# The relative-bias table of a streaming encoder step: written by one DRAM-to-DRAM broadcast, with the far bias put in by a predicated copy

## The chip, the cores and the metric

The kernel runs on one core of one Trainium2 chip. The metric is the device time of one execution in microseconds. The kernel before takes 1836.98 us (median of 3 runs, 1836.38 to 1841.36). In the profile the engines are PE (matmul) and PEld (its weight load), DVE, ACT, POOL and SP; SP and ACT also issue the transfers between DRAM and the on-chip memory, and an instruction that only issues one is marked SPq or ACTq.

## The reference, cut to what matters

One layer of an encoder runs over 512 prompt tokens and 8 x 16 sample tokens. Branch A of it is banded attention with 8 heads of 64; to each score a bias is added that depends on the head and on the clipped distance between query and key:

```python
A_MAX_REL = 128                      # 257 biases per head

def rel_bias_lookup(table, rel):
    idx = jnp.clip(rel, -A_MAX_REL, A_MAX_REL) + A_MAX_REL
    return jnp.transpose(table[idx], (2, 0, 1)).astype(jnp.float32)

# band_attn_prompt, per chunk of 64 queries and head
s = jnp.einsum('bqhd,bkhd->bhqk', qb, kb).astype(jnp.float32) * scale + bias
p = jax.nn.softmax(jnp.where(valid, s, neg), axis=-1)
```

So a key more than 128 positions back gets one constant per head, the far bias. Everything else (the projections of branches A, B and C, the gated delta rule, the state-space scan, the merge, cross attention and the feed-forward part) is the same before and after the change.

## The kernel before

The tokens lie in five tiles of 128 (four of the prompt, one of the sample). Dense products are made in three passes over a high and a low part of each operand: a weight tile of 512 KB is loaded from DRAM into a tile called `raw` (L273; two such buffers in turn), ACT makes its high part `wh` (L224, two instructions of 128x512 per tile), POOL makes its low part `wl` from both (L218, two of 128x512), and PE multiplies (L210). A `raw` buffer is free for the next load when its two `wl` are done. There are buffers for three such tiles' `wh` and for as many `wl`; a further one is free when PE has used the oldest.

The order of the program is written by generators that take turns: a list of dense units (`add`, `need`, `pump`), and beside them the steps of other work. A recording layer then puts the instructions of each engine in a row; each engine runs its row strictly in that order and waits at the head of it.

Around the change the units are: V (values of all heads, products `tm`), A0 (queries and keys of head pair 0, products `aps`, results in `aqk`), dec (a small product `dps` with 24 weight columns, loaded into a tile `rawd` that takes one of the two `raw` buffers), then A1, A2, A3 (the other head pairs; each first its queries, then its keys). The keys' result is copied from PE's memory to `aqk` by ACT and then transposed by PE (`t5a`, `t5b`). The result of `dps` goes through ACT to `dsb` and is transposed in the same way, after the first product of A1.

Between V and A0 `rel_table` (L422) makes a table in DRAM, `relt`: for each of 128 queries q and 8 heads a row of 384 numbers, 127 copies of the far bias and then the 257 biases by falling distance. The 257 columns are loaded for 8 partitions (one per head), DVE fills in the 127 copies, and one store issued from ACT writes all 128 copies of the 8 rows:

```python
self.store(self.relt.rearrange("q h c -> h q c"), t.unsqueeze(1).broadcast_to([8, P, 384]))
```

`rel_ap` (L431) reads it back with a step of one number less than a row from query to query, which yields the bias per query and key. `prompt_bias` (L1302) makes the bias tile of two heads so: a load of 128x256 from `relt`, a POOL copy that spreads column 256 (the far bias) over columns 0 to 255, and a DVE memset of the corner that is masked. It is called before the attention (for pair 0) and then once for each later pair. `attn_sample` (L1369) reads small pieces of `relt` for the sample's 16 queries and spreads the far bias in the same way (L1377).

Of the kernel before, what the change touches and what calls it, by code (L numbers as in the profile page):

```python
# [7 lines left out]
F32 = mybir.dt.float32  # L8
F32R = mybir.dt.float32r
I32 = mybir.dt.int32  # L10
# [9 lines left out]
NT = 5            # token tiles: 4 of the prompt, 1 with the 8 x 16 sample tokens  # L20
# [5 lines left out]
NEG = -3.0e38  # L26
FA, FS, FB, FC, FP, FX = 0.3, 0.85, 0.95, 1.8, 1.2, 0.5
NGA, NGB, NGC = 5, 3, 5    # gates of the branches done ahead
# [4 lines left out]
SEQ = (0, 1, 2, 4, 3)   # tiles of a group's scan  # L33
LQ = 1
SKA = 3           # softmax tiles ahead of their products
MAGIC = float(0x5F3759DF)

NU = 41           # working slots of 128 x 640
NQ = 16           # of 128 x 128
NW = 6            # half weight tiles, and as many for the low parts  # L40
NS = 17           # small slots


class Enc:
# [39 lines left out]
    # Dense products come as units (generators that yield the time their products hold the tensor  # L84
    # engine); the steps of other work yield how much dense work is to be put behind them.
# [3 lines left out]
    def tick(self):  # L89
        """Next step of the work behind every finished product."""  # L90
        self.posts = [p for p in self.posts if next(p[1], self) is not self]
        for name in [n for n in self.ended if all(p[0] != n for p in self.posts)]:
            self.ended.remove(name)
            self.done.add(name)

    def post(self, gen):
        """First step of the work behind a product; the others come with later products."""
        if gen is not None and next(gen, self) is not self:
            self.posts.append((self.units[0][0] if self.units else None, gen))
# [34 lines left out]
    def weave(self, *gens, lead=0):  # L134
        """Steps of the generators in turn, the first one lead steps ahead."""
# [14 lines left out]
    def fmj(self, wk, X, post, m=P, c=0, nm="fm", split=False):  # L150
        """A weight-stationary product and the steps behind it."""
# [16 lines left out]
    def tmj(self, wk, X, cb, tiles=range(NT), nm="tm", t0=0, late=False):  # L168
        """cb(pair, ps[128 tokens, j, 256]): X^T (weights), per pair of token tiles; X starts at tile t0.
        late: the last row block comes after the others of the first two pairs."""  # L170
# [33 lines left out]
    def load2(self, out, in_):  # L204
        """A load that does not queue behind those of the weights."""
        self.nc.sync.dma_start(out, in_)

# [24 lines left out]
    def split(self, h, l, x, eng=None):  # L232
        """x = h + l exactly, both with 12 significant bits."""
        self.act(h, x)
        self.tt(l, x, h.bitcast(F32), ALU.subtract, eng)

    def rsqrt(self, v_in, scale, eps, post=1.0):
        """post / sqrt(v_in * scale + eps), elementwise on a small tile."""
# [18 lines left out]
    def sumsq(self, x, acc):  # L257
        """acc[p] = sum over the free axis of x*x."""
# [5 lines left out]
    def weights(self, w, c0, width, k0, nk, engs=None, loose=False):  # L264
        """Columns c0..c0+width of row blocks k0..k0+nk as [(h, l)] per row block."""
# [46 lines left out]
    def masks(self):  # L312
        nc = self.nc
        self.one = self.ones("one")
        self.mi = self.ones("mi")                             # [k, i] = 1 for k <= i
        self.keep(self.mi, [[1, P]], 0, -1)
        self.ms, blk = self.ones("ms"), self.Q("blk")         # [k, j] = 1 for k > j, within blocks of 16
# [7 lines left out]
        self.blkc = self.C("blkc", [P, 8])                    # [token, b] = 1 in block b  # L325
# [4 lines left out]
    def levels(self):  # L330
        """[j, i] = 1 where i lies in the upper half and j in the lower half of one block of 2s."""
        nc = self.nc
        self.par = self.C("par", [P, 2])                      # parity of the block of 16
        nc.vector.tensor_reduce(self.par, self.blkc.rearrange("p (a c) -> p c a", c=2), axis=AX.X, op=ALU.add)
        # packed: the diagonal blocks of 32 side by side
# [22 lines left out]
    def loads(self):  # L358
        """Loads of the small parameters and the convolutions' states."""
        I = self.I  # L360
        # vectors over features
# [14 lines left out]
        # parameters per head, on all partitions  # L376
# [16 lines left out]
    def params(self):  # L393
        nc = self.nc
        # vectors transposed; conv taps and gate gains come halved
# [26 lines left out]
    def rel_table(self):  # L422
        """DRAM scratch [q, head, 384]: 127 times the far bias, then the biases by falling distance; read
        with a partition step one short of a row it yields the band's bias per (query, key)."""
        self.relt = self.dr.tile([P, 8, 384], F32, name="relt")
        t = self.U("rel", shape=(8, 384))
        self.load(t[:, 127:384], self.I["a_rel_rev"])
        self.nc.vector.tensor_copy(t[:, 0:127], t[:, 127:128].broadcast_to([8, 127]))
        self.store(self.relt.rearrange("q h c -> h q c"), t.unsqueeze(1).broadcast_to([8, P, 384]))

    def rel_ap(self, h, nq, c0, n):  # L431
        """[nq, n]: bias of query q and key column c0 + c, column 128 being the query tile's first key."""
        return bass.AP(tensor=self.relt.tensor, offset=self.relt.offset + h * 384 + 127 + c0,
                       ap=[[8 * 384 - 1, nq], [1, n]])

# [9 lines left out]
    def XT(self, nm):  # L445
        """Feature-major halves of all tokens: [(h, l)] per feature tile."""
# [3 lines left out]
    def token_norm(self, xs):  # L450
        """[128, n]: 1 / rms of the tokens of n tiles, each given as two halves."""
# [7 lines left out]
    def inv_rms(self, ss):  # L459
        """[128, n]: 1 / rms from the parts' sums of squares, [128, parts, n]."""  # L460
# [20 lines left out]
    def norm_tile(self, x, r, g):  # L481
        """Normalized halves of a token tile, transposed to psum: yields (j, psum [128, 4, 128])."""
# [8 lines left out]
    def norm_T(self, x, gain, to, groups=((0, 1), (2, 3), (4,))):  # L491
        """x[t]: two [128, 512] tiles; fills the feature-major halves of all tokens."""
# [25 lines left out]
    def conv(self, ps, key, f, hist, taps, bias, lt):  # L518
        """ps: [128, 2, 320] pre-conv; returns views (prompt, sample) of x/2 of the conv result.
        The streams' last tokens, their new state, go to column lt[1] of the batch lt[0] of lt[2]."""  # L520
# [35 lines left out]
    def store_conv(self, lt, cols, hist, op, os):  # L556
        """The batch's new states: row (f, token) of the prompt, then (f, stream, token)."""
# [12 lines left out]
    def decays(self, X):  # L570
# [4 lines left out]
        # 24 columns count, 8 more fill up a quarter of the array  # L575
        for c, c0, n in ((0, 3072, 8), (8, 6152, 16), (24, 3080, 8)):
            self.load(raw[:, :, c:c + n], wv[:, :, c0:c0 + n])
        # a quarter of the array for every two row blocks; their sums come with the transposes
# [15 lines left out]
    def decays_post(self, sb):  # L594
# [6 lines left out]
        # beta = sigmoid  # L601
# [3 lines left out]
        # softplus(x) = max(x, 0) + log1p(exp(-|x|)), log1p(e) = 2 atanh(e / (2 + e))  # L605
# [24 lines left out]
        # sums of the decays: up to a token, after a token, whole tile  # L630
# [27 lines left out]
        # the sums up to a token once more, a row per head, to be read by all partitions  # L658
# [6 lines left out]
    def decay(self, out, ts, hs, eng=None):  # L665
        """out[j, i], the sums of the decays up to token i for tiles ts or heads hs, become the decays from
        token j to i, where i >= j (and at most 1 elsewhere)."""
# [8 lines left out]
    def tr5(self, src, cols=None):  # L676
        """src(t) -> [128, 128]; returns two psum tiles, prompt [128, 512] and sample [128, 128]."""
# [7 lines left out]
    def gdn_dense(self, h, X):  # L685
# [7 lines left out]
        def post(kind):  # L693
            f = kind * 4 + h

            def run(ps):
                c = self.silu_conv(ps, "b", f, 3, [self.vc("bcw", i * 12 + f) for i in range(4)], None,
                                   (lt, kind, 3), "bc")
                if kind < 2:
                    # k and q stay as they are: what their l2 norms would scale goes by token  # L700
# [17 lines left out]
                if kind == 0:  # L718
# [3 lines left out]
                    self.stt(sc[:, 0, :], ss[:, NT:], EPS, rk, ALU.add, ALU.mult)       # 1 / rk  # L722
# [23 lines left out]
        for kind in (1, 0, 2):                                # k, q, v  # L746
# [4 lines left out]
    def gdn_solve(self, h):  # L751
        """Decays, both products with the keys, and the inverse of I + strictly upper part."""
# [11 lines left out]
        # decays between the tokens of a tile, [j, i]  # L764
# [28 lines left out]
        # E = (I + U)^-1 for U = strictly upper part, by doubling the block size; up to 32 on the diagonal  # L793
        # blocks alone, which lie packed side by side
# [24 lines left out]
        for i in range(1, 5):  # L819
            n = NT if i < 4 else 4                            # the sample's blocks are of 16 tokens  # L820
# [8 lines left out]
        # the blocks above the diagonal: -A^-1 B D^-1  # L829
# [34 lines left out]
    def gdn_run(self, h):  # L864
        """Per tile: w = E^T z, outputs and state; then norm over the head and gate."""
# [11 lines left out]
        # z = v - e^gc (k s0), w = E^T z, o = e^gc (q s0) + M^T w, state  # L877
# [60 lines left out]
        # norm over the head, gate, to feature-major halves  # L938
# [997 lines left out]
```

## Time and profile before

| | us |
|---|---|
| median of 3 runs | 1836.98 |
| range of the runs | 1836.38 to 1841.36 |
| span of the profiled execution, first to last instruction | 1828.0 |
| PE busy in it | 1727.6 (95%) |
| DVE, ACT, POOL busy | 866.0, 652.7, 612.5 |

For the profiled execution the profile gives the span alone; the runs' median lies 9.0 us above it, which is what stands around the first and the last instruction. A row of a timeline begins with its start and its duration in us; a bracket at its end gives how long the engine sat idle before it and who ended that. The chain of waits is followed back from the last instruction: each piece is the work, or the transfer, that held the end at that moment. [...] A DMA share is the mean busy share of 16 DMA engines.

### The profile page before, as it was taken

To read this page: it belongs to the slowest core of one execution; us is meant where nothing else is said; L and a number is where in the kernel's file an instruction comes from. 1 tells how busy PE (TensorE), PEld (TensorE's weight loads), DVE (VectorE), ACT (ScalarE), POOL (GpSimd) and SP (SyncE) were. 2 spreads that over 40 slices of the span, in tenths; PEclk is the share of its full clock that TensorE was granted. 3 is DMA by queue.
4 is the path that set the end of the run, shared out by engine and by line. 5 is a ranking of instruction groups with operands and counts; after the bars stand their busy time and mean duration, and the time that the engine had idled before them with its cause. 6 is when DMAs were issued, how large, how long until landed. Compare 5 with 4: busy or idle time off the path is not lost.

```text
span 1828.0 us, 34046 instructions
## 1 busy us (share of the span) xinstructions
PE 1727.6 (95%) x13705; PEld 1593.3 (87%) x13705; DVE 866.0 (47%) x1778; ACT 652.7 (36%) x1611; POOL 612.5 (34%) x644
## 2 busy tenths in 40 slices
PE   6589999999999999999999899999989999999997
PEld 6587777889888887988989899987689999999997
DVE  5034655255777674665544463342474413431433
ACT  4034444432533442343342255332433312321333
POOL 4151222212332353453333236211144433433433
PEclk9889999999999999999999999999989999999999
DMA  5341127522221343234223435146332222222322
GB/s 156 64 113 54 49 70 243 184 67 61 78 76 52 98 121 115 72 110 133 78 68 92 138 126 164 58 162 230 105 93 82 70 71 81 75 66 70 93 77 76
DMA packets 239308, 182.41 MB, mean 100 GB/s; under 512 B 13313, under 2 KB 211982, under 8 KB 239150
## 3 DMA queue, kind: packets, MB, share of 16 engines
q1 hardware_dynamic: 216192, 164.69, 29.2%
q10 hardware_dynamic: 22958, 15.54, 3.3%
q8 instruction: 108, 1.77, 0.4%
q14 instruction: 50, 0.41, 0.1%
HBM read 162.04 MB, written 16.58 MB: 98 GB/s over the span
## 4 chain that ended last, share of the span: by engine, by line
PE 78%; DVE 10%; DMA 5%; ACT 3%; issue 2%; POOL 1%; ACTq 0%; SPq 0%; POOLq 0%; DVEq 0%
PE ups L210 8%; PE fps L210 8%; PE gps L210 8%; PE dn L210 8%; PE pps L210 6%; PE ap L210 6%; PE tm L210 4%; PE bps L210 4%; PE qps L210 3%; DMA raw<-in_w_in_dram 3%; PE cps L210 2%; PE aps L210 2%; DVE xc L221 2%; DVE t L218 1%; PE asp L210 1%
## 5 line engine op out<-in xcount | busy, mean ns | idle before, releaser
L218 POOL TENSOR_TENSOR wl<-raw,wh 128x512 fp32r<-128x512 f32 x376 | 494.5, 1323 | 1029.1 <-ACT wh L224 761.3
L224 ACT ACTIVATE wh<-raw 128x512 fp32r<-128x512 f32 x400 | 248.3, 629 | 606.2 <-PE dn L210 94.3
L210 PE MATMUL dn<-wh,hh 128*128 128x256 f32 x440 | 125.1, 284 | 0.4
L210 PE MATMUL dn<-wl,hh 128*128 128x256 f32 x440 | 124.7, 283 | 0.5 <-POOL wl L218 0.5
L210 PE MATMUL dn<-wh,hl 128*128 128x256 f32 x440 | 124.5, 283 | 0.0
L210 PE MATMUL gps<-xTh,wh 128*128 128x320 f32 x448 | 114.7, 333 | 1.8 <-DVE tg L221 1.8
L221 DVE SCALAR_TENSOR_TENSOR xc<-xp,vec,xc 128x664 f32<-128x664 f32 (+1 forms) x116 | 113.9, 982 | 3.1
L210 PE MATMUL gps<-xTl,wh 128*128 128x320 f32 x448 | 106.0, 314 | 0.0
L210 PE MATMUL gps<-xTh,wl 128*128 128x320 f32 x448 | 105.9, 314 | 0.0
L541 DVE TENSOR_SCALAR xc<-xp,vec 128x656 f32<-128x656 f32 (+1 forms) x34 | 32.2, 946 | 133.3 <-ACT xp L224 133.3
L210 PEld LDWEIGHTS dn<-wh,hh 128*128 128x128 f32 x440 | 84.4, 192 | 1.2 <-DVE x L218 1.0
L210 PEld LDWEIGHTS dn<-wl,hh 128*128 128x128 f32 x440 | 84.4, 192 | 0.9 <-POOL wl L218 0.9
L210 PEld LDWEIGHTS dn<-wh,hl 128*128 128x128 f32 x440 | 84.4, 192 | 0.0
L210 PEld LDWEIGHTS gps<-xTh,wh 128*128 128x128 f32 x448 | 72.9, 189 | 12.3 <-issue 9.1
L210 PE MATMUL fps<-fTh,wh 128*128 128x320 f32 x352 | 82.5, 312 | 0.0
L210 PE MATMUL fps<-fTl,wh 128*128 128x320 f32 x352 | 81.9, 310 | 0.0
L210 PE MATMUL ups<-fTh,wh 128*128 128x320 f32 x352 | 81.8, 310 | 0.0
L210 PE MATMUL fps<-fTh,wl 128*128 128x320 f32 x352 | 81.8, 310 | 0.0
L210 PE MATMUL ups<-fTh,wl 128*128 128x320 f32 x352 | 81.8, 310 | 0.0
L210 PE MATMUL ups<-fTl,wh 128*128 128x320 f32 x352 | 81.7, 310 | 0.0
L218 DVE TENSOR_TENSOR x<-x,dn 128x256 f32<-128x256 f32 x60 | 23.0, 418 | 118.5 <-PE dn L210 118.5
L210 PEld LDWEIGHTS gps<-xTh,wl 128*128 128x128 f32 x448 | 75.3, 189 | 1.7 <-issue 1.7
(517 smaller groups left out, 4620.3 us busy)
## 6 DMA issues: line engine op xcount, KB each, us to landing
raw<-in_w_in_dram SPq DMA_DIRECT2D x72, 512.0 KB
raw<-in_w_up_dram SPq DMA_DIRECT2D x44, 512.0 KB
raw<-in_w_down_dram SPq DMA_DIRECT2D x20, 512.0 KB
ck<-in_cache_attn_k_dram SPq DMA_DIRECT2D x32, 256.0 KB
cv<-in_cache_attn_v_dram SPq DMA_DIRECT2D x32, 256.0 KB
xck<-in_cache_mem_k_dram SPq DMA_DIRECT2D x32, 256.0 KB
xcv<-in_cache_mem_v_dram SPq DMA_DIRECT2D x32, 256.0 KB
raw<-in_wx_o_dram SPq DMA_DIRECT2D x14, 512.0 KB
```

The costliest lines, as they stand in the source:

```text
L210: self.nc.tensor.matmul(out, lhsT=lhsT, rhs=rhs, start=start, stop=stop)
L218: return (eng or self.nc.vector).tensor_tensor(out, a, b, op=op)
L221: self.nc.vector.scalar_tensor_tensor(out, a, s, b, op0=op0, op1=op1)
L224: self.nc.scalar.activation(out, in_, f, **kw)
L541: nc.vector.tensor_scalar(acc[:, :n], xp[:, :n], taps[0], bias, op0=ALU.mult, op1=ALU.add)
```

## The change

`rel_table` no longer goes through the on-chip memory. The table has rows of 257 numbers per head, without the 127 copies, and one transfer issued from SP reads the 8 x 257 biases (8,224 bytes) from the input and writes them 128 times to DRAM. A second transfer from SP loads the 8 far biases to all 128 partitions (`far`). What `rel_ap` now reads for keys beyond the table is the neighbouring row; `prompt_bias` overwrites it with the far bias by a DVE copy under a mask (`ms`, one where the query's number is above the key's), and POOL takes the far bias from `far` and no longer from the loaded tile. `attn_sample` picks the far bias of each partition's head out of `far` by three small DVE instructions and puts it in by a fourth. Comments are left out too.

```diff
     def rel_table(self):
-        self.relt = self.dr.tile([P, 8, 384], F32, name="relt")
-        t = self.U("rel", shape=(8, 384))
-        self.load(t[:, 127:384], self.I["a_rel_rev"])
-        self.nc.vector.tensor_copy(t[:, 0:127], t[:, 127:128].broadcast_to([8, 127]))
-        self.store(self.relt.rearrange("q h c -> h q c"), t.unsqueeze(1).broadcast_to([8, P, 384]))
+        rev = self.I["a_rel_rev"]
+        self.relt = self.dr.tile([P, 8, A_REL], F32, name="relt")
+        self.load(self.relt.rearrange("q h c -> q (h c)"), rev.rearrange("h c -> (h c)").partition_broadcast(P))
+        self.far = self.C("far", [P, 8])
+        self.load(self.far, rev[:, 0].partition_broadcast(P))
 
     def rel_ap(self, h, nq, c0, n):
-        return bass.AP(tensor=self.relt.tensor, offset=self.relt.offset + h * 384 + 127 + c0,
-                       ap=[[8 * 384 - 1, nq], [1, n]])
+        return bass.AP(tensor=self.relt.tensor, offset=self.relt.offset + h * A_REL + c0,
+                       ap=[[8 * A_REL - 1, nq], [1, n]])
...
             self.load(b[:, 256:], self.rel_ap(2 * p + h, P, 0, 256))
-            nc.gpsimd.tensor_copy(b[:, 0:256], b[:, 256:257].broadcast_to([P, 256]))
+            far = self.far[:, 2 * p + h:2 * p + h + 1]
+            nc.gpsimd.tensor_copy(b[:, 0:256], far.broadcast_to([P, 256]))
+            nc.vector.copy_predicated(b[:, 256:384], self.ms.bitcast(I32), far.broadcast_to([P, P]))
             nc.vector.memset(b[0:64, 448:512], NEG)
...
-        nc.gpsimd.tensor_copy(bc[:, 0:384], bc[:, 384:385].broadcast_to([P, 384]))
+        fr = self.SM("far8", [P, 8])
+        self.tt(fr, self.far, self.blkc, ALU.mult)
+        f1 = self.SM("far1", [P, 1])
+        nc.vector.tensor_reduce(f1, fr, axis=AX.X, op=ALU.add)
+        low = self.SM("low", [P, 16])
+        nc.vector.tensor_reduce(low, self.ms_s.rearrange("p (a c) -> p c a", c=16), axis=AX.X, op=ALU.add)
+        nc.vector.copy_predicated(bc[:, 384:400], low.bitcast(I32), f1.broadcast_to([P, 16]))
+        nc.gpsimd.tensor_copy(bc[:, 0:384], f1.broadcast_to([P, 384]))
```

The recording layer puts the two new transfers early. SP's row at the start of the program, before; `raw56` and `raw61` are the second half of V's weights, `raw99` and `raw106` those of A0:

```order
L227 DMA x13_105<-in_x_sample_dram 128x512
L227 DMA x14_107<-in_x_sample_dram 128x512
L227 DMA raw56_258<-in_w_in_dram 128x4x256
L227 DMA raw61_268<-in_w_in_dram 128x4x256
L227 DMA raw99_618<-in_w_in_dram 128x8x128
```

And now:

```order
L228 DMA x13_105<-in_x_sample_dram 128x512
L228 DMA x14_107<-in_x_sample_dram 128x512
L228 DMA relt_607<-in_a_rel_rev_dram 128x2056
L228 DMA far_609<-in_a_rel_rev_dram 128x8x1
L228 DMA raw56_258<-in_w_in_dram 128x4x256
L228 DMA raw61_268<-in_w_in_dram 128x4x256
L228 DMA raw98_617<-in_w_in_dram 128x8x128
```

Both new transfers stand ahead of the second half of V's weights, and the load of `rel` that stood behind `rawd` is gone.

ACT's row from the end of V to the transposes of A0's keys, before (`wh107`, `wh109`: A0's keys; `wh136`, `wh138`: A1's queries; `wh151`, `wh153`: A1's keys; `aqk104`, `aqk111`: the results of A0's queries and keys):

```order
L224 ACTIVATE wh107_683<-raw106_681 128x512
L224 ACTIVATE wh109_687<-raw106_681 128x512
L230 DMA relt_607<-rel94_608 8x128x384
L224 ACTIVATE V87_345<-tm93_580 128x256
L224 ACTIVATE aqk104_676<-aps98_617 128x640
L230 DMA out_12_dram<-V87_345 128x512
L224 ACTIVATE wh136_852<-raw135_850 128x512
L224 ACTIVATE wh138_856<-raw135_850 128x512
L224 ACTIVATE wh151_954<-raw150_952 128x512
L224 ACTIVATE wh153_958<-raw150_952 128x512
L224 ACTIVATE aqk111_739<-aps105_680 128x640
L224 ACTIVATE ktm114_749<-t5a112_742 128x512
```

And now (`wh135`, `wh137` and `wh150`, `wh152` for A1; `wh157`, `wh159`: A2's queries, loaded as `raw156`):

```order
L225 ACTIVATE V87_345<-tm93_580 128x256
L231 DMA out_12_dram<-V87_345 128x512
L225 ACTIVATE wh135_853<-raw134_851 128x512
L225 ACTIVATE wh137_857<-raw134_851 128x512
L225 ACTIVATE aqk103_675<-aps97_616 128x640
L225 ACTIVATE wh150_955<-raw149_953 128x512
L225 ACTIVATE wh152_959<-raw149_953 128x512
L225 ACTIVATE wh157_1017<-raw156_1015 128x512
L225 ACTIVATE wh159_1021<-raw156_1015 128x512
L225 ACTIVATE aqk110_738<-aps104_679 128x640
L225 ACTIVATE ktm113_748<-t5a111_741 128x512
```

The store of `relt` is gone, and one more weight tile, A2's queries, now stands ahead of the result of A0's keys.

ACT's row a little later, around the result of `dps`, before:

```order
L224 ACTIVATE vec1_797<-vps129_795 128x88
L224 ACTIVATE wh158_1016<-raw157_1014 128x512
L224 ACTIVATE wh160_1020<-raw157_1014 128x512
L224 ACTIVATE dsb133_847<-dps132_814 128x640
L224 ACTIVATE aqk148_947<-aps134_849 128x640
```

And now:

```order
L225 ACTIVATE vec1_796<-vps128_794 128x88
L225 ACTIVATE wh168_1111<-raw167_1109 128x512
L225 ACTIVATE wh170_1115<-raw167_1109 128x512
L225 ACTIVATE dsb132_848<-dps131_815 128x640
L225 ACTIVATE aqk147_948<-aps133_850 128x640
```

The weight tile ahead of `dsb` is now A2's keys, one tile further on, whose `wh` take the buffers that A1's queries hold. On PE the order of the units is unchanged.

## Rows read from the trace of the kernel before

**Rows 1.** The page: the span, and busy time (share of the span) of each engine.

```profile
span 1828.0 us, 34046 instructions
PE 1727.6 (95%) x13705; PEld 1593.3 (87%) x13705; DVE 866.0 (47%) x1778; ACT 652.7 (36%) x1611; POOL 612.5 (34%) x644
```

**Rows 2.** Chain of waits in order of time: start, us, what held the end.

```profile
55.76 31.75 DMA raw<-in_w_in_dram
...
88.30 2.50 POOL wl L218 x2
...
90.81 3.62 DMA raw<-in_w_in_dram
...
94.52 1.15 ACT wh L224 x2
95.66 0.60 ACT aqk L224
...
96.31 1.11 PE t5a L215 x4
...
1084.97 4.41 DMA raw<-in_wx_k_dram
```

**Rows 3.** Timeline of ACT, from the store of the table to A1.

```profile
53.29 0.55 ACTq L230 DMA_DIRECT2D relt<-rel  x1
...
87.59 1.15 ACT L224 ACTIVATE wh<-raw 128x512 fp32r<-128x512 f32 x2 [25.16 <-DMA raw<-in_w_in_dram]
...
103.61 0.71 ACT L224 ACTIVATE dsb<-dps 128x640 f32<-128x640 f32 x1 [0.40 <-PE dps L210]
...
118.18 0.63 ACT L224 ACTIVATE wh<-raw 128x512 fp32r<-128x512 f32 x1 [2.90 <-PE aps L210]
```

**Rows 4.** Timeline of PE, around the longest idle time at the start.

```profile
68.66 1.26 PE L210 MATMUL dps<-xTh,rawd 128*32 128x320 f32 x10
96.31 1.11 PE L215 MATMUL t5a<-ident,aqk 128*128 128x128 f32 x4 [26.38 <-ACT aqk L224]
```

**Rows 5.** Stretches: window, us, PE busy (instructions), granted clock, DMA share, GB/s.

```profile
4.00:6.00 2.00, 0.00 (x0) 1.00 0.81 198
10.00:17.00 7.00, 5.48 (x25) 1.00 1.05 372
70.00:74.00 4.00, 0.00 (x0) 1.00 0.48 62
...
96.30:101.30 5.00, 4.99 (x35) 0.50 0.47 120
101.30:103.50 2.20, 2.20 (x35) 0.99 0.79 255
```

**Rows 6.** DMA from 53.2 to 87.6 us: queue with packets, MB, share; issue with KB.

```profile
q10 hardware_dynamic: 1169, 1.83, 43.0%
...
relt<-rel ACTq DMA_DIRECT2D x1, 1536.0 KB
```

**Rows 7.** DMA from 31 to 36 us, the many-packet loads of `rawd`: SP's queue.

```profile
q1 hardware_dynamic: 3573, 0.16, 43.6%
```

**Rows 8.** DMA from 671 to 677 us, two broadcast loads `dx`: SP's queue.

```profile
q1 hardware_dynamic: 349, 0.56, 32.5%
```

**Rows 9.** The page: packets that load instructions, over the whole span.

```profile
q8 instruction: 108, 1.77, 0.4%
```

**Rows 10.** Timeline of SP: issues of the second half of V's weights and of A0's.

```profile
12.03 12.74 SPq L227 DMA_DIRECT2D raw<-in_w_in_dram  x4
```

**Rows 11.** Timeline of POOL: low parts of that half of V's weights, and of A1's.

```profile
17.91 6.48 POOL L218 TENSOR_TENSOR wl<-raw,wh 128x512 fp32r<-128x512 f32 x4 [3.41 <-ACT wh L224]
...
88.30 2.49 POOL L218 TENSOR_TENSOR wl<-raw,wh 128x512 fp32r<-128x512 f32 x2 [32.57 <-ACT wh L224]
```

**Rows 12.** Timeline of DVE: four row normalisations of V's tokens beside that POOL work.

```profile
17.45 5.80 DVE L221 SCALAR_TENSOR_TENSOR xn<-x,y,grow 128x512 f32<-128x512 f32 x4
```

**Rows 13.** DVE groups from 100 to 270 us: a three-operand instruction of 128x128.

```profile
L221 DVE SCALAR_TENSOR_TENSOR bc<-bc,xc 128x128 f32<-128x128 f32 x4 | 1.1, 286 | 0.0
```

More of the change, by code (lines that the diff above doesn't have):

```diff
@@ L26 @@
 NEG = -3.0e38
+A_REL = 257
 FA, FS, FB, FC, FP, FX = 0.3, 0.85, 0.95, 1.8, 1.2, 0.5
```

## Prediction, made before the changed kernel ran

> **What bounds the kernel now.** I read the page first: PE is busy for 95% of the span [rows 1], so a change that takes nothing from PE's row can only win where PE stands still. The change touches the first 270 us, so the second view is the chain of waits over that stretch, looked through for its longest piece. That is one load of a weight tile, A1's queries, 31.75 us long [rows 2]. The same kind of load takes 3.62 us a little later in the same chain, and 4.41 us where it is slow [rows 2]. The third view is ACT's timeline: the store of the table is issued at 53.29, 2.5 us ahead of that load, and ACT then stands for 25.16 us until the load lands [rows 3]. The fourth is PE's: it runs out of work at 68.66 + 1.26 = 69.9 and gets the transposes of A0's keys only at 96.31, after 26.38 us [rows 4]. What it waits for is not the load itself but `aqk`, which stands in ACT's row behind the `wh` of two loads that have not come.
>
> Why the load is late is in the DMA rows. While nothing but the store and the load are under way (70 to 74 us), the share is 0.48 of 16 engines at 62 GB/s; a saturated stretch of plain loads shows 1.05 at 372 GB/s [rows 5]. Over 53.2 to 87.6 us ACT's queue took 43.0% of 16 engines x 34.4 us = 237 engine-us for 1,169 packets [rows 6]. The store has 8 x 128 = 1,024 rows of 1,536 bytes; with some 0.1 us for each of the other 145 packets it is left with about 0.22 us a row, 7 GB/s per engine. On 8 engines that is 128 x 0.22 = 28 us, and the load's parts on those engines wait for it. So the store from eight partitions is the cause, and its time is nearly all of the 31.75 us.
>
> **The change part by part.** I follow the steps to the moment at which PE restarts.
>
> The store goes. Its load is issued at 55.76 as before, when the previous tile's low part is done, and now lands after 3.62 us. But the gain isn't the whole wait, because ACT's new row puts a third tile ahead of `aqk`, and `rawd` holds one of the two buffers, so the three loads run one after another: each waits until the tile ahead of it is split. From a landing to the next issue took 90.81 - 87.51 = 3.30 us, and from the last landing (94.43) to PE's start 1.88 us [rows 2]. New start: 55.76 + 3 x 3.62 + 2 x 3.30 + 1.88 = 75.1. The store of V's last tile (256 KB) now goes out beside the first load; at 372 GB/s [rows 5] that is 0.7 us, so 75.8. PE still stands, but for 5.9 us and not 26.4: **-20.5 us**. With loads of 4.41 us it would be 2.4 us less.
>
> The new transfers are not free: SP's row has them ahead of the second half of V's weights, in a stretch where the DMA engines are saturated (1.05, 372 GB/s) [rows 5], and those weights are issued behind them on the same queue [rows 10]. The table is 128 x 8,224 bytes = 1.05 MB. No row shows a DRAM-to-DRAM transfer. From below, 1.05 MB at 372 GB/s is 2.8 us. From above, two broadcast loads, which also read the same bytes for all partitions, moved 0.56 MB in 6 us, 93 GB/s [rows 8]: 11.3 us. In between stand the first loads of the program, the broadcast of the norm's gains among them, at 198 GB/s [rows 5]: 5.3 us; and packets of 1.77 MB / 108 = 16 KB that took 0.4% of 16 x 1,828 = 117 engine-us, 1.08 us each [rows 9], which gives 4.3 us for the 8 rows of 8 KB that each of 16 engines has. I take 4.3, as the nearest in packet size and in reading from DRAM in long rows. `far` is 1,024 pieces of 4 bytes; the loads of `rawd` and small ones with them show 3,573 packets in 43.6% of 16 x 5 us = 34.9 engine-us, 9.8 ns each [rows 7]: 0.6 us. So V's weights come 4.9 us later. Part of it comes back: POOL took 6.48 us for their four low parts [rows 11] while DVE worked on its normalisations until 23.25 [rows 12]; two such parts alone took 2.49 us [rows 11]. Started 4.9 us later, at 22.8, the four take 5.0 us. Everything up to A0 hangs on it: **+3.5 us**, with bounds of 2.0 and 10.5.
>
> Sixteen engines for the new table is my assumption; with 8 it would take 8.6 us, inside the bounds. The rows show 8 for the store, whose outermost dimension is 8. [...]
>
> A new wait behind `dps`: the `wh` that now stands ahead of `dsb` belong to A2's keys, and the second of them needs the buffer that A1's queries hold until their product ends. PE's next work after that product is the transpose of `dsb`. Before, `dsb` was copied at 103.61, right behind `dps`, while PE was still busy with A1's queries [rows 3]. Now PE waits for one `wh` (0.63, a row where it also waits for PE) and `dsb` (0.71) [rows 3]: **+1.4 us** with the hand-over. Queued behind it on ACT is only the next copy of `aqk`, and nobody needs that earlier.
>
> The predicated copies: none is in the trace. Below, 0; a three-operand instruction of 128x128 takes 0.286 us [rows 13], so 8 are 2.3 us, twice that if the mask costs a pass. Two lie in the decays' work of DVE, which is done well before PE asks. Six stand between softmax steps, where PE has other products to do; DVE is 47% busy [rows 1]. The load that they wait for is the one that the memset behind them waited for already. With the four small ones for the sample I take **+0.5 us**, between 0 and 2.5.
>
> At no cost: POOL's copies, which now need `far` alone and lie a little earlier; the DVE fill and the load that went; ACT's store.
>
> [...]
>
> Sum: -20.5 + 3.5 + 1.4 + 0.5 = -15.1. The profiled span of 1828.0 becomes 1812.9. The median of the runs stands 9.0 us above that span, which the change doesn't touch: 1836.98 - 15.1 = 1821.9, so 1822.
>
> **The rivals.**
> *The broadcast is slow at the start.* If all engines read one row of DRAM as slowly as in the two broadcast loads (11.3 us), the start costs 10.5 and not 3.5 us: 1829. For it: that row is the only pure broadcast. Against: those transfers are smaller and have rows of 2 KB, so their landing weighs more.
> *The table blocks V's weights for longer than the store blocked A1's.* The place is the same queue, at 12 us, with nothing for PE behind it. It turns slower when the table holds the engines for more than 4.3 + 15.1 = 19.4 us, a rate below 54 GB/s. The store had 62 GB/s [rows 5]; at half of that, since every byte is now read from DRAM and written to it, the table takes 34 us and the time is 1851. Against: the packets of 16 KB ran at 15 GB/s per engine, 240 GB/s for 16.
> *The store is not the cause.* Then the load stays late, nothing is won, and the time is 1837 + 5.4 = 1842. Against: the rate and share of those 30 us.
> *More is won.* A table at the saturated rate, no fall of the clock and hidden copies: -21.2 + 2.0 + 1.4 - 2.5, about 1817.
>
> **How the numbers follow.** Forecast (1818 to 1826): 0.65. Slow broadcast, 1826 to 1831: 0.17. More won, below 1818: 0.06. Ended within 0.3% (a table near the break-even): 0.06. Blocking table or wrong cause: 0.06. A measurement of this kernel can tell 0.3%, 5.5 us, from no change. The first three are faster, 0.88; one to two in a hundred of the slow broadcast reaches over the line, so 0.87, 0.07 and 0.06. The range takes the forecast, nearly all of the slow broadcast and some of the better end: 1816 to 1830.
>
> **What would show it.** PE's idle time before the transposes of A0's keys falls from 26.4 to about 6 us; their start is near 79. The load of A1's queries takes about 4 us. The four low parts of V's second half start near 22.8 and not 17.9, and PE waits there. PE waits 1.4 us between A1's queries and the transposes of `dsb`. No predicated copy stands in the chain for more than 1 us together. The forecast is wrong if the table holds the engines for much more than 5 us, or if a wait for the third tile is longer than two splits and three loads make it.

## The result, and the profile after

The changed kernel takes **1821.22 us** (median of four runs, 1815.74 to 1822.53) beside 1836.99 for the kernel before in the same session: a ratio of 0.9909, 95% interval 0.9889 to 0.9929, some 16 us less. In a later session it took 1817.34 (1815.33 to 1820.07) beside 1836.45, ratio 0.9898 (0.9880 to 0.9915), 19 us less. Three executions of all, at 2,774, 3,317 and 7,334 us, are far above the others and are left out of every median and ratio here. The first profile of after, against [rows 1]:

```profile
span 1820.8 us, 34050 instructions
PE 1735.3 (95%) x13705; PEld 1599.9 (88%) x13705; DVE 865.1 (48%) x1789; ACT 652.8 (36%) x1611; POOL 610.4 (34%) x644
```

No engine's busy time falls by more than 2.1 us, and PE's is even 7.7 higher; in the second profiles of before and after it is 1736.2 and 1732.3, so this is no cost of the change. What went is PE's idle time at the start. The chain of waits (start, us, what held the end), against [rows 2]:

```profile
60.41 3.94 DMA raw<-in_w_in_dram
...
65.14 2.57 POOL wl L219 x2
...
67.73 3.85 DMA raw<-in_w_in_dram
...
72.37 2.52 POOL wl L219 x2
...
74.90 3.81 DMA raw<-in_w_in_dram
...
79.96 0.60 ACT aqk L225
...
80.61 1.11 PE t5a L216 x4
...
82.28 6.05 PE dps L211 x54
...
95.99 0.60 ACT dsb L225
```

The load of 31.75 us is gone. In its place stand three loads of 3.8 to 3.9 us, one after another, with a split between them. PE's timeline (start, us, work, in brackets the idle time before it), against [rows 4]:

```profile
73.31 1.26 PE L211 MATMUL dps<-xTh,rawd 128*32 128x320 f32 x10
80.61 1.11 PE L216 MATMUL t5a<-ident,aqk 128*128 128x128 f32 x4 [6.03 <-ACT aqk L225]
...
96.64 0.66 PE L216 MATMUL t5a<-ident,dsb 128*128 128x128 f32 x4 [1.08 <-ACT dsb L225]
```

PE idles for 6.03 us and not 26.38, but reaches `dps` at 73.31 and not at 68.66; ahead of the transposes of `dsb` it idles for a new 1.08 us. Stretches (window, us, busy times, granted clock, DMA share, GB/s), against [rows 5]:

```profile
10.00:17.00 7.00, 5.51 (x25) 4.82 (x24) 2.90 (x12) 4.84 (x13) 4.81 (x4) 1.00 1.05 398
...
80.60:85.60 5.00, 4.99 (x35) 2.71 (x39) 0.27 (x1) 1.17 (x4) 1.42 (x2) 0.50 0.44 105
```

The table goes out in the first of these, at a DMA share of 1.05 and 398 GB/s. After the 6 us wait the granted clock, as a share of full speed, is 0.50 for 5 us, as it was after the long one [rows 5]. POOL's low parts of V's second half, against [rows 11]:

```profile
21.33 4.98 POOL L219 TENSOR_TENSOR wl<-raw,wh 128x512 fp32r<-128x512 f32 x4 [6.52 <-ACT wh L225]
```

They start 3.4 us later than before and take 4.98 us and not 6.48. The predicated copies on DVE over the whole span (count, busy us, mean ns, idle time before them and what ended it):

```profile
L1313 DVE COPY_PREDICATED bias<-ms,far 128x128 f32<-128x128 int32 x8 | 3.2, 407 | 11.9 <-DMA bias<-relt 11.9
```

Eight take 3.2 us together, and none stands in the chain of waits.

### The profile page after: what moved, and what is told of

It is laid out like the page before. It is cut to its first block, busy times and chain, and to the rows that moved or that the text cites. A ratio compares the mean times of both kernels' runs of the same rounds, so it can differ in the third digit from the quotient of the medians.

```text
span 1820.8 us, 34050 instructions
## 1 busy us (share of the span) xinstructions
PE 1735.3 (95%) x13705; PEld 1599.9 (88%) x13705; DVE 865.1 (48%) x1789; ACT 652.8 (36%) x1611; POOL 610.4 (34%) x644
## 4 chain that ended last, share of the span: by engine, by line
PE 78%; DVE 11%; DMA 4%; ACT 3%; issue 2%; POOL 1%; ACTq 0%; SPq 0%; POOLq 0%; DVEq 0%
PE ups L211 8%; PE fps L211 8%; PE gps L211 8%; PE dn L211 8%; PE pps L211 6%; PE ap L211 6%; PE tm L211 4%; PE bps L211 3%; PE qps L211 3%; PE cps L211 2%; PE aps L211 2%; DVE xc L222 2%; PE asp L211 1%; PE apo L211 1%; DVE t L219 1%
## 5 line engine op out<-in xcount | busy, mean ns | idle before, releaser
L211 PEld LDWEIGHTS gps<-xTl,wh 128*128 128x128 f32 x448 | 75.2, 189 | 2.1 <-issue 2.1
```

The source lines that it names most:

```text
L211: self.nc.tensor.matmul(out, lhsT=lhsT, rhs=rhs, start=start, stop=stop)
```

## Experiments

**The kernel before once more**, for a second profile.

> The kernel before once more, for a second profile. Theory (the profile that the prediction was made on is a quick execution: its span lies 4 to 8 us under the spans of the runs): span 1832 to 1838; the four low parts of V's second half start at 19.0, as in the three other kernels with no table ahead of V's weights, and not at 17.91; run time and span differ by 1.7 to 1.8 us. Rival (9 us stand around the span, as the prediction says): span 1828, run time 1837.

1840.28 us beside 1837.83 for the other runs of before in that session, ratio 1.0009 (0.9987 to 1.003). The profiled run took 1840.99 at a span of 1839.2: 1.8 us lie around the span, not 9. The span is a little above the 1832 to 1838 expected, and POOL's four low parts start at 18.60, between the two values. PE's timeline:

```profile
71.72 1.26 PE L210 MATMUL dps<-xTh,rawd 128*32 128x320 f32 x10
99.64 1.12 PE L215 MATMUL t5a<-ident,aqk 128*128 128x128 f32 x4 [26.66 <-ACT aqk L224]
```

The idle time is that of [rows 4], but `dps` starts 3.1 us later. In the five other kernels below that keep the old store it starts between 71.40 and 72.02. So the profile behind the prediction is of a quick execution, by 3 us at this place. The clock goes with it. From 15 to 60 us (PE's busy time, clock, DMA share, GB/s), the first profile of before has

```profile
15.00:60.00 45.00, 40.15 (x298) 0.96 0.35 86
```

and its repeat

```profile
15.00:60.00 45.00, 40.33 (x280) 0.89 0.31 79
```

Both profiles of after have 0.89 here, and no other run above 0.92. By an estimate from these rows, 0.07 of 45 us is 3.1 us of work at the full clock, about the whole difference.

**The changed kernel once more.**

> The changed kernel once more, for a second profile and more times. Theory: the gain is the stall ahead of the transposes of A0's keys, and the 15.7 us by which they start earlier (96.31 to 80.61) stay to the end, but for the wait ahead of dsb; then the median is again near 1821, and the places at which the first profile gave back 8 us later (a cache load near 336 us, the scan near 681, two weight loads near 1096) differ from profile to profile. Rival: the give-back belongs to the change (a lost overlap further down); then the same places show the same losses in this profile, and the shift at the end is again near 7 us.

1817.34 us, as told. PE's timeline:

```profile
73.77 1.26 PE L211 MATMUL dps<-xTh,rawd 128*32 128x320 f32 x10
81.07 1.11 PE L216 MATMUL t5a<-ident,aqk 128*128 128x128 f32 x4 [6.04 <-ACT aqk L225]
```

The median is 3.9 us below that of the first session and so not near 1821. Against the repeat of before `dps` is 2.05 us later and the transposes are 18.57 us earlier. The start cost and the stall repeat; what the first pair of profiles gave back later does not. Near 1,060 to 1,130 us the chain of the first profile of after waits for two slow loads, and for two of 3.4 us:

```profile
1075.87 6.08 DMA raw<-in_wx_k_dram
...
1095.10 6.11 DMA raw<-in_wx_v_dram
```

That of the repeat waits for this one alone:

```profile
1059.27 3.37 DMA raw<-in_wx_k_dram
```

Neither version touches these loads, and in the repeat of before one takes 6.15 us too. Two profiles of one kernel differ by several us in such places; the first pair's 7.2 us (1828.0 to 1820.8) is no measure of the change.

**The copies alone.**

```diff
+        self.far = self.C("far", [P, 8])
+        self.load(self.far, self.I["a_rel_rev"][:, 0].partition_broadcast(P))
...
-            nc.gpsimd.tensor_copy(b[:, 0:256], b[:, 256:257].broadcast_to([P, 256]))
+            far = self.far[:, 2 * p + h:2 * p + h + 1]
+            nc.gpsimd.tensor_copy(b[:, 0:256], far.broadcast_to([P, 256]))
+            nc.vector.copy_predicated(b[:, 256:384], self.ms.bitcast(I32), far.broadcast_to([P, P]))
```

> The kernel before with one part of the change alone: far is loaded and put in by the predicated copies, the table of 384 columns and its store from eight partitions stay. Theory (the store is the cause): 1837 to 1839, the load of A1's queries still takes over 30 us, PE still waits about 26 us. Rival (the gain comes from the copies, from POOL's fill no longer waiting for the loaded tile, or from the order of the rows): 1822 to 1830.

1836.42 us, ratio 1.0005 (0.999 to 1.002). The load of A1's queries takes nearly as long as before:

```profile
58.79 30.84 DMA raw<-in_w_in_dram
```

PE still idles for 25.62 us. The copies neither win nor cost anything that can be measured, so the gain isn't theirs; that the store was the cause is shown by the spread rows below.

**The broadcast issued later**, behind A0's weights.

```diff
-        self.rel_table()
         self.need("A0")
         with self.tc.issue_after(self.last_raw.ins):
+            self.rel_table()
             self.loads()
```

> The changed kernel with the broadcast and far issued behind A0's weights instead of ahead of the second half of V's. Theory (the broadcast costs the start, because V's weights queue behind it): the fourth low part of V's weights ends near where it did in the kernel before, the transposes of A0's keys start 4 to 5 us earlier, at 76 to 77, and the time falls by 3.5 to 5 us, to about 1817. Rival (the start is later for another reason, or the broadcast only moves its cost to rawd and A1's queries): 1820 to 1823, within 1 us of the changed kernel.

1818.44 us, ratio 0.9901 (0.9882 to 0.992): no change against 1817.34. `dps` starts at 71.97 and the transposes at 79.03, 2.0 us earlier than in the repeat of after and not 4 to 5. POOL's low parts start at 19.05 (22.12 in the repeat of after). So the broadcast does hold up V's weights, but it costs 2 us at `dps`, and the medians of four runs don't resolve 2 us.

**Four tables instead of one.**

```diff
+        for i in range(3):
+            more = self.dr.tile([P, 8, A_REL], F32, name=f"more{i}")
+            self.load(more.rearrange("q h c -> q (h c)"), rev.rearrange("h c -> (h c)").partition_broadcast(P))
```

> The changed kernel with four tables written instead of one, all ahead of the second half of V's weights: three more DRAM-to-DRAM broadcasts of 1.05 MB, to price one. If one runs at the saturated rate of the loads (372 GB/s, 2.8 us): V's weights land 8.5 us later and the time is 1817 plus 6 to 8.5 us, 1823 to 1826. If one takes the 4.3 us of the prediction: 12.9 us later, 1828 to 1830. At the 93 GB/s of the small broadcast loads (11.3 us): 34 us later, 1850.

1826.28 us, ratio 0.9945 (0.9928 to 0.9962), 8.9 us more than the repeat of after for three tables. SP's timeline shows the third one behind V's weights, not ahead of them:

```profile
11.58 0.60 SPq L228 DMA_DIRECT2D relt<-in_a_rel_rev_dram  x1
12.26 1.20 SPq L228 DMA_DIRECT2D more<-in_a_rel_rev_dram  x2
13.68 1.83 SPq L228 DMA_DIRECT2D raw<-in_w_in_dram  x2
15.56 5.69 SPq L228 DMA_DIRECT2D more<-in_a_rel_rev_dram  x1
```

POOL's low parts, here and in the repeat of after:

```profile
28.31 5.45 POOL L219 TENSOR_TENSOR wl<-raw,wh 128x512 fp32r<-128x512 f32 x4 [13.22 <-ACT wh L225]
```

```profile
22.12 4.98 POOL L219 TENSOR_TENSOR wl<-raw,wh 128x512 fp32r<-128x512 f32 x4 [6.46 <-ACT wh L225]
```

So two more tables hold V's weights up by 6.2 us and one by some 3.1, near the 2.8 of the saturated rate, 372 GB/s in [rows 5] (`far` is issued behind the weights here, so its cost, 0.6 us by the prediction's estimate, is not in the 6.2). At `dps` only 2.8 us are left of the 6.2 (76.56 to 73.77). Where the rest of the 8.9 us arises was not found.

**Rows spread over the partitions, everything else as before.** The eight rows stand on partitions 0, 16, ..., 112 and then on 0, 4, ..., 28 in place of 0 to 7; the store still has eight rows outermost.

```diff
-        t = self.U("rel", shape=(8, 384))
-        self.load(t[:, 127:384], self.I["a_rel_rev"])
+        t = self.U("rel", shape=(P, 384))
+        self.load(t[:, 127:384], self.I["a_rel_rev"].unsqueeze(1).broadcast_to([8, 16, 257]))
...
-        self.store(self.relt.rearrange("q h c -> h q c"), t.unsqueeze(1).broadcast_to([8, P, 384]))
+        self.store(self.relt.rearrange("q h c -> h q c"), t[::16].unsqueeze(1).broadcast_to([8, P, 384]))
```

> The kernel before with the eight rows of the table on partitions 0, 16, ..., 112 and every engine's row in the order of before (the earlier run with the spread rows had also moved the copy of A0's keys on ACT, which by itself won 5.6 us). Theory (neighbouring partitions make the store slow): the load of A1's queries takes 16 to 18 us and not 31, the transposes of A0's keys start 13 to 14 us earlier than in the run with the copies alone, at 84 to 86, and the time is 1821 to 1825. Rival (the order made most of that run's gain): 1830 to 1837.

1824.07 us, ratio 0.9932 (0.9913 to 0.995). Its chain and the stretch from 62 to 70 us:

```profile
58.50 17.07 DMA raw<-in_w_in_dram
...
84.62 1.11 PE t5a L215 x4
```

```profile
62.00:70.00 8.00, 8.00 (x57) 8.00 (x56) 0.44 (x2) 0.70 (x1) 0.00 (x0) 1.00 0.53 123
```

The share is still near a half, that of eight engines (0.53; 0.48 in [rows 5]; which eight, it does not say), but they carry 123 GB/s and not 62.

> The kernel before with the eight rows of the table on partitions 0, 4, ..., 28 and every engine's row in the order of before. The runs so far: rows on 0 to 7 carry 62 GB/s, rows on 0, 16, ..., 112 carry 124 GB/s, on the same eight engines. [...] Rival (what matters is how far the rows lie apart): the load takes 16 to 31 us and the time is 1823 to 1837.

1814.85 us (1806.57 to 1819.27), ratio 0.9871 (0.9846 to 0.9895). Its chain:

```profile
58.71 9.09 DMA raw<-in_w_in_dram
...
76.91 0.66 PE t5a L215 x4
```

The load is down from 31 to 9.1 us, and rows 4 apart are quicker than rows 16 apart, so the rival falls: it is not the distance that counts, but which partitions are read. From 63 to 65 us the run carries 201 GB/s at a share of 0.58, beside 123 at 0.53 for the rows 16 apart and 62 at 0.48 for rows 0 to 7. What makes one set of partitions slower than another no run shows. At the saturated rate of [rows 5] a share of 0.58 would carry, by an estimate from that row, 372 x 0.58 / 1.05 = 205 GB/s, so here the eight engines may be the limit and no longer the partitions.

**ACT's row.** The first spread version (the tile zeroed by DVE instead of being loaded for all partitions) had also changed the order.

> The kernel before, with the eight rows of the table on partitions 0, 16, ..., 112 instead of 0 to 7; the store still has eight rows as its outermost dimension and so, if the rows of before carry over, eight engines. Theory A (a transfer on eight engines is slow as such, 0.22 us per packet of 1,536 bytes whatever it reads): no change, 1836 to 1839, A1's queries still land after 30 us. Theory B (eight neighbouring partitions share a way out of the on-chip memory): packets take about half as long or less, the store about 14 us, A1's queries land some 14 to 20 us earlier and the time is 1817 to 1824.

1811.84 us, ratio 0.9869 (0.9851 to 0.9887). ACT's timeline:

```profile
71.55 0.70 ACT L224 ACTIVATE aqk<-aps 128x640 f32<-128x640 f32 x1 [6.33 <-PE aps L210]
75.39 1.15 ACT L224 ACTIVATE wh<-raw 128x512 fp32r<-128x512 f32 x2 [3.14 <-DMA raw<-in_w_in_dram]
```

The time is below the range of both theories. The result of A0's keys is copied ahead of the `wh` that wait for a load, so PE doesn't wait for it: from 66 to 112 us PE's only idle time is 0.52 us ahead of the transposes of `dsb`. This run mixes two causes. The order by itself, in the kernel before and in the changed one:

```diff
+            def wk():
+                if (p, j) in FIRST:
+                    with self.tc.issue_after(self.keys0):
+                        return self.weights(w, j * 512 + p * P, P, 0, NK)
+                return self.weights(w, j * 512 + p * P, P, 0, NK)
-            yield from self.fmj(lambda: self.weights(w, j * 512 + p * P, P, 0, NK), X, post(j), nm="aps")
+            yield from self.fmj(wk, X, post(j), nm="aps")
```

`keys0` is the copy of A0's keys to `aqk`, behind which the `wh` of the tiles named in `FIRST` are queued on ACT: A1's queries and keys in the kernel before, A1's keys and A2's queries in the changed one.

> The kernel before, table and store unchanged, with one thing moved: on ACT the copy of A0's keys to aqk stands ahead of the high parts of A1's weights (as the run with the spread rows had it by accident). Theory (the slow store alone makes the load late, but PE stands only because aqk is queued behind the wh of that load): the load of A1's queries still takes about 31 us; the transposes of A0's keys start at 72 to 76 and not at 96 to 99, dps follows at once, and PE then waits for A1's queries from about 80 to 91; since the transposes and dps (8 to 9 us) and one load with its split (6.9 us) leave the path, 1822 to 1826, most of the change's gain without touching the store. Rival (PE needs A1's weights anyway, so the wait only moves to them): 1833 to 1837.

1831.51 us, ratio 0.9975 (0.9961 to 0.9988): about 5 us won, not 11 to 15. PE's timeline, and the chain:

```profile
73.22 0.66 PE L216 MATMUL t5a<-ident,aqk 128*128 128x128 f32 x4
...
91.53 0.90 PE L211 MATMUL aps<-xTh,wh 128*128 128x320 f32 x2 [13.47 <-ACT wh L225]
...
103.48 0.56 PE L211 MATMUL aps<-xTh,wh 128*128 128x320 f32 x2 [2.23 <-ACT wh L225]
```

```profile
59.12 31.66 DMA raw<-in_w_in_dram
...
98.43 3.98 DMA raw<-in_w_in_dram
```

The transposes come at once, as expected, but the load of A1's keys now stands behind thirteen small loads in SP's row and is issued at 98.43: the load that I took off the path stayed on it. With the slow store, this move, with that side effect on SP's row, is worth a quarter to a third of the change.

> The changed kernel with the same move on ACT: the copies to aqk stand behind the high parts of A1's queries and ahead of those of A1's keys and A2's queries. Theory (the 6.0 us that PE still idles ahead of the transposes and the 1.1 us ahead of dsb come from that place in ACT's row, not from a load that PE needs): both waits go, 1817 less 6 to 7 us, 1810 to 1812. Rival (PE then waits as long for A1's queries or keys, whose loads run one after another because rawd holds a buffer): 1815 to 1818.

1809.27 us, ratio 0.985 (0.9832 to 0.9868), 8 us under the repeat of after. The chain is PE's own work:

```profile
74.36 1.19 PE dps L212 x10
75.55 0.59 PE t5a L217 x4
...
76.43 3.90 PE dps L212 x54
80.33 7.24 PE aps L212 x48
87.57 0.44 PE t5a L217 x4
```

Both waits are gone, and the clock no longer falls there (1.00 from 60 to 100 us): the 54 products of `dps` take 3.90 us in place of 6.05 in the first profile of after.

> The same move on ACT with the broadcast and far issued behind A0's weights. Against the run before it in this list it prices the place of the broadcast once more. Theory after the first late run and its comparison with the kernel that has the copies alone (PE at 40 us: 2.1 us later with the table early, 0.0 later with the table late): 1 to 3 us less, 1808 to 1811. Rival (V's weights do not hang on the table): the same time within 1 us.

1808.56 us, ratio 0.9846 (0.9829 to 0.9862), the quickest version here. In its profile `dps` starts at 71.22 and not at 74.29, but 0.7 us between the medians is less than they resolve, so it decides nothing between theory and rival.

**rawd in a tile of its own.** The loads of `rawd` are also tied behind A0's weights, and ACT's row differs as told in the expectation.

```diff
-        raw = self.wp.tile([P, 8, 32], F32, name="rawd", tag="raw", bufs=2)
+        self.dex = self.C("dex", [P, 312])
+        raw = self.dex[:, 0:256].rearrange("p (k c) -> p k c", k=8)
```

> The changed kernel with rawd in a tile of its own (the constant that later holds the decays' exponentials), so that both raw buffers serve weight tiles; ACT's row has A1's two tiles' high parts ahead of A0's queries' result, and dsb ahead of A2's keys. Theory (the three loads that the prediction adds up run one after another only because rawd holds a buffer): A1's two loads then run at once, the transposes wait 0 to 3 us and not 6.0, dsb does not wait, 1810 to 1815. Rival (the loads' number ahead of aqk decides, whatever buffers there are): 1816 to 1820.

1813.01 us (three executions), ratio 0.9875 (0.9843 to 0.9906). Its chain:

```profile
73.91 1.20 PE dps L211 x10
75.10 0.59 PE t5a L216 x4
...
86.91 0.63 ACT wh L225
87.54 0.60 ACT dsb L225
...
88.19 0.66 PE t5a L216 x4
```

The 6 us ahead of the transposes are gone; 1.1 us ahead of `dsb` stay, because in its row too, against the expectation, the `wh` of A2's keys came first. The three serial loads of the prediction were a matter of buffers, and could be cured there or by ACT's order.

## Why the prediction held, term by term

The forecast was 1822, with 1816 to 1830; the runs gave 1821.2 and 1817.3.

- **The stall, -20.5.** PE idled 26.38 and then 6.03 us: -20.35 (26.66 to 6.04 in the repeats: -20.62). The three loads in series took 3.94, 3.85 and 3.81 us; splits and hand-overs came as worked out. That the load was late by the store is shown by the spread rows.
- **The start, +3.5.** +2.1 (`dps` at 71.72 and 73.77 in the repeats). Size wrong, direction right. V's weights came 3.5 us later (POOL at 18.60 and 22.12) and not 4.9: a table takes some 3.1 us, not 4.3. It ran at nearly the saturated rate, the lower bound in the text; the row that I called nearest, the packets that load instructions, was too slow. The upper bound of 93 GB/s [rows 8] counts idle time too: in the first two of those 6 us all queues together carried 209 and 240 GB/s. The catch-up on POOL (4.98 us in place of 6.5) came as predicted. That the table uses sixteen engines, on which the 4.3 rests, was my assumption, and no run shows it by itself; 1.05 MB in 3.1 us is some 340 GB/s, more than the 201 at a share of 0.58 above, and from 10 to 17 us, while it goes out, the share is 1.05 of sixteen engines.
- **dsb, +1.4.** 1.08 us, in both profiles of after.
- **The copies, +0.5.** Nothing that the runs can tell: 1.0005 (0.999 to 1.002), and none in the chain.
- **The clock.** The sum has no term for it; the 2.5 us in "more is won" are an estimate, half of the 5 us at 0.50 in [rows 5]. PE's clock was 0.50 for 5 us after the short wait as after the long one, so nothing was gained there. At the start the repeats of before and after have the same clock, 0.89 from 15 to 60 us, so nothing was lost there either; only the first profile of before had a higher one, 0.96.
- **The sum.** -15.1 predicted; the terms as measured give -20.6 + 2.1 + 1.1 = -17.4, and the medians moved by 15.8 and by 19.1. With the measured terms the forecast would have been 1819.6. The two sessions' medians are 3.9 us apart and lie on either side of it, so the mechanism held, but that 1821.2 is within 1 us of 1822 is luck.
- **A wrong step that did no harm.** The text puts 9.0 us around the span. The runs have 1.7 to 1.8; the profiled execution was about 7 us under the median of the runs. A difference added to a median doesn't see that, but a time added up from that span would have been 7 us too short. "Near 79" for the transposes came out as 80.6 and 81.1: the 3 us by which that profile was quick, less the 1.4 us that were too much in the start.
- **A cause named too broadly.** The text blames eight partitions by way of eight engines at 7 GB/s each. At a share near a half, that of eight engines, 62 GB/s went with rows 0 to 7, 123 with the rows 16 apart and, at 0.58, 201 with those 4 apart. The gain doesn't need the way from DRAM to DRAM: the old store with rows four partitions apart gives 1814.85.

Of the rivals, the slow broadcast and the blocking table fall with 3.1 us a table; "the store is not the cause" falls with the spread rows. Of "more is won" (1817) the faster table and the hidden copies came true and the clock did not; that the later session's median is 1817.34 lies within the scatter between sessions.

## What to carry to other kernels

When an engine waits, follow its queue back: here PE waited for a copy that needed no load but was queued on ACT behind work that did, and moving that copy won 8 us on top of the faster table. Price a store from few partitions by which partitions it reads, not by its engines alone: the load behind this one took 31.75, 17.07 and 9.09 us with its eight rows on three sets of partitions, at DMA shares of 0.48, 0.53 and 0.58. And take a second profile of the unchanged kernel before a term of 3 us is read from a pair of profiles.

## What was not expected of the hardware

In one profile, part of what the waits had given was lost again to the clock. In the changed kernel with the new order, which has PE busy for all of the 70 us from 60 to 130, the clock is at 0.50 for longer at the small products here (stretches of 4 us, PE's busy time first, clock third from the end):

```profile
116.00:120.00 4.00, 4.00 (x22) 2.98 (x22) 1.36 (x11) 1.23 (x6) 0.00 (x0) 0.50 0.70 192
120.00:124.00 4.00, 4.00 (x14) 3.31 (x15) 0.76 (x5) 0.41 (x2) 0.00 (x0) 0.50 0.03 9
```

and in the repeat of after at the same place of the program:

```profile
128.00:132.00 4.00, 4.00 (x18) 3.67 (x18) 0.96 (x7) 1.01 (x3) 0.00 (x0) 0.61 0.01 2
```

Up to this place the new order was 9.6 us ahead of the repeat; past it, 6.9 us. That the missing wait is the reason is not shown: in the first profile of before the clock stays at 1.00 there, and in its repeat, after the same long wait, it falls to 0.50 as well (144 to 148 us). Why it falls longer in one run was not tried.
